# Opening of the first feed-forward part in groups of 2, 3, 4 and 7 row blocks, with every conditioning pass placed behind a low part of the weights

## Chip, cores and metric

The kernel runs on one core of one Trainium2 chip. The metric is the device time of one execution in microseconds, lower is better; three executions of the kernel before give a median of 2366.59 us (2357.86 to 2370.3). Besides these there is one profiled execution, whose trace is read below.

## What is computed

A decoder layer for 256 positions of width 2048: a SwiGLU feed-forward part (width 5632), a pair of token mixers (retention and sliding-window attention), a second feed-forward part, a last norm. Each of the three parts first norms its input and then scales and shifts it by numbers made from a conditioning vector `c`; each result is gated the same way. All weights are fp32 and are used once.

```python
SEQ, D_MODEL, D_FF = 256, 2048, 5632
mod = silu(c) @ w_ada + b_ada            # 9 outputs of 2048: shift, scale, gate for each part
x = x + 0.5 * gate1 * swiglu(modulate(rms_norm(x), shift1, scale1), w_ffn1_gu, w_ffn1_down)
h = modulate(rms_norm(x), shift2, scale2)
x = x + gate2 * token_mixing(h, w_in, w_ret_branch, w_swa_branch, w_out)
x = x + 0.5 * gate3 * swiglu(modulate(rms_norm(x), shift3, scale3), w_ffn2_gu, w_ffn2_down)
return rms_norm(x)
```

(The lines are condensed from the reference.)

## The kernel before

**Weights.** A weight load puts 4 row blocks of 128 by 512 columns (128x2048 numbers, 1 MB) into a buffer `raw`; there are four of them. `load` (L351) issues it on SP's queue. A load is used in two *pieces* of 2 row blocks. For each piece ScalarE (ACT) casts the high part `wh` (`split`, L375), VectorE (DVE) subtracts to get the low part `wl` (L377), and TensorE (PE) does 12 matmuls (`products`, L360): activations high by weights high, low by high, high by low, for 2 row blocks and 2 halves of the positions. The pool that holds `wh` and `wl` has three buffers of each. A `raw` comes free when the low parts of both its pieces are made.

**Conditioning.** One output of `w_ada` (m = 0 to 8) is a sum over 16 rows (k = 0 to 15), each of 128x2048 numbers or 1 MB. A row is loaded on SP's queue (`ada_load`, L215) and multiplied by `silu(c)` and summed on DVE in quarters (`ada_pass`, L220: one pass over 128x512 and a short instruction that reads the sum). Outputs 1 and 0 are needed at once; the others are made later by the generator `conditioning`: after each piece `tick` adds the rate to a counter and takes as many *steps* as are due; a step is one quarter pass, and it asks for the loads of the rows that lie up to `ahead` steps ahead. For outputs 2, 4 and 3 that makes 192 steps; during the rest of the first feed-forward part (`ffn_up`, `down_product`) 1.094 steps come to a piece. During the mixing they are 0.95 to a piece (outputs 7, 6, 5), and in the second feed-forward part 0.43 (output 8). Rows go into a *ring* of two (`two_rows`): row i takes the half that row i-2 had, so its load must wait for the last quarter pass of row i-2.

**What sets the order.** SP's queue is in the order of the program (`manual_schedule`), and an instruction of it that waits holds up everything behind it, weights too. The other engines are ordered by a scheduler, which may pull an instruction ahead of its place in the program; `tc.issue_after(x)` keeps an instruction behind `x`.

**Opening.** The first feed-forward part needs shift and scale of all 16 row blocks of its input. Its first 16 weight chunks (`chunks`) are therefore visited four times, each time with a group of row blocks whose shift and scale are done (`bounds`, `group`, `visit`); meanwhile `group` makes those of the next. Between visits the partial sums lie in SBUF: ACT moves them there (`to_parts`, L1219) and seeds PSUM with them at the next visit (`open_banks`, L1191).

The profile shows these times of the stages: groups at 27 to 65, 65 to 155, 155 to 286 and 286 to 373 us; the rest of the first feed-forward part to about 740 us; then the mixing, in which rows in the ring `rows_x` are used from 1140.1 to 1486.2 us.

Of the kernel before, what the change touches and what calls it, by code (L numbers as in the profile page):

```python
# [9 lines left out]
F32 = mybir.dt.float32  # L10
# [3 lines left out]
ALU = mybir.AluOpType  # L14
# [3 lines left out]
P = 128  # L18
# [59 lines left out]
def layer_kernel(  # L78
# [55 lines left out]
    def t512():  # L134
        return tmp.tile([P, CH], F32, tag="t512", name=nm("t"))
# [4 lines left out]
    def slot():  # L140
        return slots.tile([P, KD * S], F32, tag="slot", name=nm("slot"))
# [69 lines left out]
    def ada_load(m, k, w, loads=1):  # L211
        src = w_ada[(m * KD + k) * P : (m * KD + k + 1) * P, :]
        for i in range(loads):
            at = slice(i * D // loads, (i + 1) * D // loads)
            nc.sync.dma_start(w[:, at], src[:, at])  # L215

    def ada_pass(k, w, sums, q, passes=AQ):

        at = slice(q * D // passes, (q + 1) * D // passes)
        nc.vector.tensor_tensor_reduce(  # L220
            out=w[:, at],
            in0=w[:, at],
            in1=cact[:, at],
            scale=1.0,
            scalar=0.0,
            op0=ALU.mult,
            op1=ALU.add,
            accum_out=sums[:, k, q : q + 1],
        )
# [17 lines left out]
    def raw_row():  # L247
        raw = raws.tile([P, KB, CH], F32, tag="raw", name=nm("raw"))
        return raw.rearrange("p k n -> p (k n)")

    def two_rows(both=None):

        both = slot() if both is None else both
        turn = [both[:, :D], both[:, D:]]

        def place():
            turn.append(turn.pop(0))
            return turn[-1]

        return place  # L260
# [5 lines left out]
    def conditioning(outputs, place, behind):  # L266


        tiles = [(m, k) for m, _, _ in outputs for k in range(KD)]
        held = {}  # L270
        step = 0
# [361 lines left out]
    def parts_of_h(held, k, h):  # L633

        h = h.rearrange("p (k s) -> p k s", s=S)
        nc.scalar.copy(held.hi[:, k : k + 2, :], h)
        nc.vector.tensor_sub(held.lo[:, k : k + 2, :], h, held.hi[:, k : k + 2, :].bitcast(F32))

    def add_gated(bank, t, c0, gate, ssq):

# [338 lines left out]
    rows_of, alone = {}, [False]  # L979

    def place(m, k):
        if k < 1:
            rows_of[m, k] = raw_row()
        else:
            if not alone[0]:
                ring.reverse()
            rows_of[m, k] = ring[0]
        ada_load(m, k, rows_of[m, k], 2 if k < 2 else 1)

# [33 lines left out]
            op0=ALU.mult, op1=ALU.add, accum_out=dest,  # L1023
        )

    def turned_x(k0):

        xn = [t512()[:, : 2 * P] for _ in range(NT)]
        for t in range(NT):
            nc.scalar.mul(xn[t], x_sb[:, t, k0 * P : (k0 + 2) * P], r[:, t : t + 1])  # L1030
        turned = [bank()[:, :S] for _ in range(2)]
        for i in range(2):
# [22 lines left out]
    def normed_columns(k0):  # L1055

        xt = t512()
        both = xt.rearrange("p (k s) -> p k s", s=S)
        nc.sync.dma_start(both, x_t[k0 : k0 + 2].rearrange("k p s -> p k s"))
        nc.gpsimd.tensor_tensor(  # L1060
            out=both, in0=both, in1=root_row[0][:, None, :].broadcast_to([P, 2, S]), op=ALU.mult
        )
        return [xt[:, i * S : (i + 1) * S] for i in range(2)]

    def group(ks, passes=2):

        for k0 in ks[::2]:
            srcs = normed_columns(k0) if k0 >= TURNED else None
            for k in (k0, k0 + 1):
                for m in (1, 0):  # L1070
                    if (m, k) not in rows_of:
                        place(m, k)
                    for q in range(passes):
                        ada_pass(k, rows_of[m, k], early[m], q, passes)
                    yield
            for m in (1, 0):
                ada_end(m, slice(k0, k0 + 2), early[m], 0 if m else None, passes)
            h = t512()
            for i, src in enumerate(srcs or turned_x(k0)):
                modulated(h[:, i * S : (i + 1) * S], k0 + i, src, 0)  # L1080
            parts_of_h(held, k0, h)

    banks, moved, unlinted, fresh = {}, set(), set(), set()
    for n, one_bank in zip(firsts, (acc_bank, side_bank)):
        banks[n] = [one_bank() for _ in range(NT)]

# [17 lines left out]
    with tc.manual_schedule(engines=ORDERED):  # L1104
# [87 lines left out]

    def visit(n, ks, ends, ticks=False, ends_all=False):
        if n not in prepared:
            begin(n, ks)
        if n not in banks:
            open_banks(n, not ends_all)
        for make, part in prepared.pop(n):
            a, b = part[0] - ks[0], part[-1] + 1 - ks[0]
            hl = slice(part[0], part[-1] + 1)  # L1200
            wh, wl = make()
            products(
                banks[n],
                held.hi[:, hl, :],
                held.lo[:, hl, :],
                wh,
                wl,
                n in fresh and a == 0,
                b == len(ks) and ends,
                seeded=n in unlinted,  # L1210
            )
            if ticks:
                tick()
        fresh.discard(n)

    def to_parts(n):
        for p, b in zip(part_of(n), banks.pop(n)):
            with tc.issue_after(cast[-1]):
                nc.scalar.copy(p, b)  # L1219
        moved.add(n)  # L1220

    ROWS_FFN1 = [(2, None, 0.5), (4, 1, None), (3, None, None)]
# [2 lines left out]
    def place_row():  # L1225
        return row_ring[0]() if row_ring else raw_row()

    def place_early():
        if row_ring:
            return row_ring[0]()  # L1230
        return ring[1] if alone[0] else raw_row()

    for g, ks in enumerate(groups):
        alone.append(g == len(groups) - 2)
        del alone[:-1]
# [533 lines left out]
```

## Time and profile before

| | before |
|---|---|
| three executions: median (range) | 2366.59 us (2357.86 to 2370.3) |
| profiled execution: time / span | 2357.64 us / 2355.5 us |
| granted TensorE clock | 0.999 |
| instructions PE matmul / DVE / ACT | 10445 / 2576 / 1888 |
| HBM read over the span | 598.47 MB |
| conditioning rows loaded: into slots / `rows_x` / `raw` | 87 / 31 / 22 |

The page gives for each engine its busy time within the span; the span is what the profiler recorded of the execution, and the time of the execution lies 2.1 us above it. The longest idle times of the other engines (ACT's cast waiting for PE: 752.6 us in 555 waits) are those of engines that run ahead and wait for buffers.

### The profile page before, as it was taken

Reading aid. Unit: us, or ns where it says so; the run is one execution under the profiler, and the core shown is the slowest. Engines: PE = TensorE matmul, PEld = TensorE weight load, DVE = VectorE, ACT = ScalarE, POOL = GpSimd, SP = SyncE. Lnnn points to the kernel's source line nnn. Section 1 sums busy time; section 2 is a strip of 40 time slices with the busy share of each in tenths; the row PEclk is TensorE's granted clock in tenths of the full one; section 3 lists DMA queues with packets and bytes.
Section 4 is the critical chain, followed back from the end, with each engine's and each line's share of the span. In section 5 each row is a group of like instructions: output and inputs, shape, how many; then the busy total and the mean of one; then the engine's idle time right before and its main releaser. Section 6 shows DMA issues by size and latency. Waiting matters only on the chain.

```text
span 2355.5 us, 28357 instructions
## 1 busy us (share of the span) xinstructions
PE 2335.7 (99%) x10445; PEld 1918.6 (81%) x10445; DVE 1673.1 (71%) x2576; ACT 1367.2 (58%) x1888; POOL 18.3 (1%) x27
## 2 busy tenths in 40 slices
PE   8999999999999999999999999999999999999998
PEld 5888888888888888778888888888888888888887
DVE  7788888778867768976777776676555555555656
ACT  6766567455556567774556564465455454455544
POOL 0000000000000000000000000000000000000000
PEclk9999999999999999999999999999999999999999
DMA  9989889988765889876778787754767768666553
GB/s 383 375 323 361 355 294 328 336 306 293 302 237 220 293 267 255 258 212 254 267 273 306 288 310 281 272 204 179 259 237 256 242 239 268 223 231 202 193 197 125
DMA packets 191901, 630.24 MB, mean 268 GB/s; under 512 B 113105, under 2 KB 114769, under 8 KB 121233
## 3 DMA queue, kind: packets, MB, share of 16 engines
q1 hardware_dynamic: 189266, 617.41, 74.6%
q0 software_dynamic: 1600, 9.83, 1.0%
q8 instruction: 82, 1.34, 0.2%
q10 hardware_dynamic: 896, 1.19, 0.1%
q14 instruction: 57, 0.47, 0.1%
HBM read 598.47 MB, written 4.22 MB: 256 GB/s over the span
## 4 chain that ended last, share of the span: by engine, by line
PE 96%; DMA 2%; DVE 1%; ACT 1%; issue 0%; SPq 0%; DVEq 0%; ACTq 0%
PE pa L360 93%; DMA raw<-in_w_ffn_gu_dram 1%; DMA rows_x<-in_w_ada_dram 1%; PE ps L1453 0%; DVE slot L220 0%; PE pd L1369 0%; DVE wl L377 0%; ACT wh L375 0%; DMA x_sb<-in_x_dram 0%; PE ps L360 0%; PE pa L1099 0%; PE ps L895 0%; PE pd L1099 0%; DVE rows_x L220 0%; PE ps L1369 0%
## 5 line engine op out<-in xcount | busy, mean ns | idle before, releaser
L377 DVE TENSOR_TENSOR wl<-raw,wh 128x1024 fp32r<-128x1024 f32 x792 | 963.5, 1225 | 511.0 <-ACT wh L375 451.6
L375 ACT CAST wh<-raw 128x1024 fp32r<-128x1024 f32 x792 | 830.6, 1054 | 818.7 <-PE pa L360 752.6
L360 PE MATMUL pa<-wh,hh 128*128 128x512 f32 x2184 | 597.0, 391 | 3.0 <-ACT wh L375 1.7
L360 PE MATMUL pa<-wh,hl 128*128 128x512 f32 x2184 | 592.6, 389 | 0.0
L360 PE MATMUL pa<-wl,hh 128*128 128x512 f32 x2184 | 586.2, 390 | 0.2
L360 PEld LDWEIGHTS pa<-wh,hh 128*128 128x128 f32 x2184 | 407.5, 188 | 91.6 <-ACT wh L375 2.9
L360 PEld LDWEIGHTS pa<-wl,hh 128*128 128x128 f32 x2184 | 409.4, 188 | 86.7 <-DVE wl L377 1.0
L360 PEld LDWEIGHTS pa<-wh,hl 128*128 128x128 f32 x2184 | 409.8, 188 | 86.1 <-issue 0.4
L360 PE MATMUL pa<-wh,a 128*128 128x512 f32 x1824 | 452.1, 389 | 0.0
L360 PEld LDWEIGHTS pa<-wh,a 128*128 128x128 f32 x1824 | 341.7, 188 | 70.6
L360 PE MATMUL pa<-wl,a 128*128 128x512 f32 x912 | 245.1, 389 | 0.0
L220 DVE CUSTOM_DVE_ANT_0 slot<-slot,cact 128x512 f32<-128x512 f32 (+2 forms) x288 | 219.3, 812 | 30.0 <-DMA slot<-in_w_ada_dram 29.5
L360 PEld LDWEIGHTS pa<-wl,a 128*128 128x128 f32 x912 | 171.1, 188 | 35.4
L551 ACT COPY slot<-back 128x512 uint16<-128x512 uint16 x148 | 98.7, 766 | 0.0
L220 DVE CUSTOM_DVE_ANT_0 rows_x<-rows_x,cact 128x512 f32<-128x512 f32 x124 | 78.7, 686 | 18.0 <-DMA rows_x<-in_w_ada_dram 17.8
L410 ACT CAST a<-slot 128x512 fp32r<-128x512 f32 x114 | 70.6, 620 | 29.3 <-PE pa L360 29.0
L535 ACT COPY flat<-t 128x512 uint16<-128x512 uint16 x136 | 76.7, 617 | 8.9 <-DVE t L1526 5.7
L411 DVE TENSOR_TENSOR a<-slot,a 128x512 fp32r<-128x512 f32 x114 | 77.8, 684 | 0.3 <-ACT a L410 0.3
L220 DVE CUSTOM_DVE_ANT_0 raw<-raw,cact 128x512 f32<-128x512 f32 (+1 forms) x92 | 60.7, 709 | 14.6 <-DMA raw<-in_w_ada_dram 14.5
L1219 ACT COPY slot<-pa 128x512 f32<-128x512 f32 x72 | 38.6, 589 | 21.2 <-PE pa L360 21.0
L360 PE MATMUL pa<-wh,home 128*128 128x512 f32 x160 | 39.5, 389 | 0.0
L220 DVE DVE_READ_ACCUMULATOR2_ANT sums<- 128x1 f32 x440 | 35.9, 82 | 0.0
(232 smaller groups left out, 1087.0 us busy)
## 6 DMA issues: line engine op xcount, KB each, us to landing
raw<-in_w_ffn_gu_dram SPq DMA_DIRECT2D x160, 1024.0 KB, 5.5
raw<-in_w_in_dram SPq DMA_DIRECT2D x104, 1024.0 KB, 5.8
raw<-in_w_ffn_down_dram SPq DMA_DIRECT2D x88, 1024.0 KB, 4.9
slot<-in_w_ada_dram SPq DMA_DIRECT2D x87, 1024.0 KB, 7.4
rows_x<-in_w_ada_dram SPq DMA_DIRECT2D x31, 1024.0 KB, 7.1
raw<-in_w_ada_dram SPq DMA_DIRECT2D x22, 1024.0 KB, 5.7
raw<-in_w_swa_branch_dram SPq DMA_DIRECT2D x16, 1024.0 KB, 5.0
raw<-in_w_ret_branch_dram SPq DMA_DIRECT2D x16, 1024.0 KB, 5.4
```

Of the source, the lines that this page charges most:

```text
L220: nc.vector.tensor_tensor_reduce(out=w[:, at], in0=w[:, at], in1=cact[:, at], scale=1.0, scalar=0.0, op0=ALU.mult, op1=ALU.add, accum_out= ...
L360: product = nc.tensor.matmul(banks[t], act[:, j, t * P : (t + 1) * P], weights[:, j, :], start=starts and i == 0 and j == 0, stop=ends and ...
L375: cast.append(nc.scalar.copy(hi, src).ins)
L377: low.append(nc.vector.tensor_sub(lo, src, hi.bitcast(F32)).ins)
L410: nc.scalar.copy(hi, v)
L411: nc.vector.tensor_sub(lo, v, hi.bitcast(F32))
L535: nc.scalar.copy(planes[:, i, :], words(src)[:, :, i])
L551: nc.scalar.copy(into[:, :, :, i], held["turned"][:, i])
L1219: nc.scalar.copy(p, b)
```

## The change

The groups become 2, 3, 4 and 7 row blocks, so a group may end in a single block, and a weight load in a piece of half the size. Rows of the opening get a slot of their own (`rows_home`), whose two halves always take turns. In the second group chunks 4, 7, 10 and 13 (`by_vector`; chunk 1 is also in the list, but its sums stay in PSUM) are not seeded: DVE adds the old sum afterwards. The later conditioning starts only in the last group, with half-row loads into a ring of four places, and from there on each of its passes, in the whole kernel, is placed behind `low[-1]`, the low part made last in the program's order.

```diff
-    def two_rows(both=None):
+    def two_rows(both=None, parts=2):
         both = slot() if both is None else both
-        turn = [both[:, :D], both[:, D:]]
+        n = 2 * D // parts
+        turn = [both[:, i * n : (i + 1) * n] for i in range(parts)]
+        if parts == 2:
+            turn.reverse()
...
+        def ask(at):
+            (m, k), q = tiles[at // AQ], at % AQ
+            w = place()
+            n = min(w.shape[1] * AQ // D, AQ - q)
+            w = w[:, : n * D // AQ]
+            c0 = q * D // AQ
+            nc.sync.dma_start(
+                w, w_ada[(m * KD + k) * P : (m * KD + k + 1) * P, c0 : c0 + n * D // AQ]
+            )
+            for i in range(n):
+                held[at + i] = (w, q)
+            return n
...
-                    for i in range(step // AQ, min((step + pace["ahead"]) // AQ + 1, len(tiles))):
-                        if i not in held:
-                            held[i] = place()
-                            ada_load(*tiles[i], held[i])
-                    if behind is not None and step < 2 * AQ:
-                        with tc.issue_after(behind.ins):
-                            ada_pass(k, held[step // AQ], sums, q)
-                    else:
-                        ada_pass(k, held[step // AQ], sums, q)
+                    while asked <= step + pace["ahead"] and asked < AQ * len(tiles):
+                        asked += ask(asked)
+                    w, first = held.pop(step)
+                    early_on = behind is not None and step < 2 * AQ
+                    with tc.issue_after(behind.ins if early_on else low[-1]):
+                        ada_pass(k, w, sums, q, first=first)
...
     part = [slot() for _ in range(3)]
-    tiles = [slot(), part[0]]
-    ring = [tiles[0][:, :D], tiles[0][:, D:]]
+    tiles = part[:2]
+    rows_home = slot()
+    ring = [rows_home[:, :D], rows_home[:, D:]]
...
-            if not alone[0]:
-                ring.reverse()
+            ring.reverse()
...
-    TURNED = 6
+    TURNED = 5
...
-    bounds = (0, 2, 6, 12, 16)
+    bounds = (0, 2, 5, 9, 16)
...
+        if seeded and n in by_vector:
+            added.add(n)
+            seeded = False
...
-        for make, part in prepared.pop(n):
+        for i, (make, part) in enumerate(prepared.pop(n)):
+            if ticks and i == KB // 2:
+                turn_step()
...
     def to_parts(n):
         for p, b in zip(part_of(n), banks.pop(n)):
+            if n in added:
+                with tc.issue_after(low[-1]):
+                    nc.vector.tensor_add(p, p, b)
+                continue
...
-        if g == len(groups) - 2:
-            set_pace(ROWS_FFN1, 192, place_early, 0)
+        by_vector = chunks[1::3] if g == 1 else ()
         if final:
-            pace["rate"], pace["ahead"] = 1.0, 1
+            row_ring.append(two_rows(rows_home, 4))
+            set_pace(ROWS_FFN1, 192, place_row, AQ)
...
-            visit(n, ks, n not in stay, g == len(groups) - 2 or final and i < 8, final or (g == len(groups) - 2 and n in stay))
+            visit(n, ks, n not in stay, final, final or (g == len(groups) - 2 and n in stay))
...
-    row_ring.append(two_rows())
+    row_ring[0] = two_rows(rows_home)
     pace["rate"] = (192 - 64) / 117
     pace["ahead"] = AQ
```

What is left out lets `group`, `turned_x`, `normed_columns` and `parts_of_h` take one block in place of two. After the change line 220 is 222, 351 is 368, 375 is 392, 377 is 394, 411 is 428, and the later rows are loaded by `ask` at L285 (those of the opening still at L215).

**VectorE in `down_product` of the first feed-forward part.** `wl` is a low part; a row with a slot and `cact` is a quarter pass, and the 128x1 row behind it reads its sum. The slot named is the ring. Before:

```order
L377 TENSOR_TENSOR wl_795_4545<-raw_793_4542,wh_794_4544 128x1024
L411 TENSOR_TENSOR a_787_4503<-slot_5_114,a_787_4503 128x512
L377 TENSOR_TENSOR wl_797_4563<-raw_793_4542,wh_796_4562 128x1024
L220 ISA slot_562_3115,sums_759_4330<-slot_562_3115,cact_103 128x512
L220 ISA sums_759_4330 128x1
L220 ISA slot_562_3115,sums_759_4330<-slot_562_3115,cact_103 128x512
L220 ISA sums_759_4330 128x1
L220 ISA slot_562_3115,sums_759_4330<-slot_562_3115,cact_103 128x512
L220 ISA sums_759_4330 128x1
L220 ISA slot_562_3115,sums_759_4330<-slot_562_3115,cact_103 128x512
L220 ISA sums_759_4330 128x1
L377 TENSOR_TENSOR wl_802_4588<-raw_800_4585,wh_801_4587 128x1024
```

And now:

```order
L394 TENSOR_TENSOR wl_771_4293<-raw_769_4290,wh_770_4292 128x1024
L222 ISA slot_8_117,sums_599_3229<-slot_8_117,cact_103 128x512
L222 ISA sums_599_3229 128x1
L394 TENSOR_TENSOR wl_773_4310<-raw_769_4290,wh_772_4309 128x1024
L222 ISA slot_8_117,sums_599_3229<-slot_8_117,cact_103 128x512
L222 ISA sums_599_3229 128x1
L428 TENSOR_TENSOR a_774_4327<-slot_5_114,a_774_4327 128x512
L394 TENSOR_TENSOR wl_778_4336<-raw_776_4333,wh_777_4335 128x1024
L222 ISA slot_8_117,sums_599_3229<-slot_8_117,cact_103 128x512
L222 ISA sums_599_3229 128x1
```

Before, the scheduler put the four passes of a row together, some eight pieces ahead of their place in the program; now each stands behind the low part that it has in the program, one to a piece.

**SP's queue in the same stretch.** A row with `w_ada` is a row load, one with `w_ffn1_down` a weight load; the brackets name what it waits for beyond what the queue has waited for already (DMAHW a DMA, DVE and Activation the engine's progress). Before:

```order
L351 DMA raw_736_4172<-in_w_ffn1_down_dram 128x2048 [waits DMAHW2_49,DVE_49]
L215 DMA slot_562_3115<-in_w_ada_dram 128x2048 [waits DMAHW3_49]
L351 DMA raw_742_4213<-in_w_ffn1_down_dram 128x2048 [waits DMAHW5_49,DMAHW4_49,DVE_49]
L215 DMA slot_562_3115<-in_w_ada_dram 128x2048 [waits DMAHW0_49]
L351 DMA raw_749_4256<-in_w_ffn1_down_dram 128x2048 [waits DMAHW7_49,DMAHW6_49,DVE_49]
L351 DMA raw_754_4292<-in_w_ffn1_down_dram 128x2048 [waits DMAHW1_49,DVE_49]
L215 DMA slot_562_3115<-in_w_ada_dram 128x2048 [waits DMAHW3_49]
```

And now:

```order
L368 DMA raw_750_4163<-in_w_ffn1_down_dram 128x2048 [waits DMAHW1_49,Activation_49]
L285 DMA slot_8_117<-in_w_ada_dram 128x2048 [waits DMAHW2_49,DVE_49]
L368 DMA raw_755_4200<-in_w_ffn1_down_dram 128x2048 [waits DMAHW3_49,Activation_49]
L368 DMA raw_763_4249<-in_w_ffn1_down_dram 128x2048 [waits DMAHW4_49,Activation_49]
L285 DMA slot_8_117<-in_w_ada_dram 128x2048 [waits DMAHW5_49,DVE_49]
L368 DMA raw_769_4290<-in_w_ffn1_down_dram 128x2048 [waits DMAHW7_49,DMAHW6_49,Activation_49]
```

The loads stand in the same pattern, one row to two weights (to one, now and then). What moved is the wait on DVE: before it stood at the weight loads, for the low parts that free a `raw`; now it stands at the row loads, for the last pass of the row two before.

**SP's queue in the mixing**, where rows go into `rows_x`; `back` is a transpose by DMA. Before:

```order
L215 DMA rows_x_9224<-in_w_ada_dram 128x2048 [waits DMAHW2_49]
L351 DMA raw_1778_10171<-in_w_swa_branch_dram 128x2048 [waits DMAHW3_49,DVE_49]
L351 DMA raw_1784_10214<-in_w_swa_branch_dram 128x2048 [waits DMAHW4_49,DVE_49]
L215 DMA rows_x_9224<-in_w_ada_dram 128x2048 [waits DMAHW5_49]
L540 DMA_TRANSPOSE back_1789_10251<-flat_1749_10033 128x8x128 [waits DMAHW6_49,Activation_49]
```

And now:

```order
L285 DMA rows_x_9301<-in_w_ada_dram 128x2048 [waits DMAHW4_49,DVE_49]
L368 DMA raw_1805_10248<-in_w_swa_branch_dram 128x2048 [waits DMAHW5_49,Activation_49]
L368 DMA raw_1811_10291<-in_w_swa_branch_dram 128x2048 [waits DMAHW6_49,Activation_49]
L285 DMA rows_x_9301<-in_w_ada_dram 128x2048 [waits DMAHW7_49,DVE_49]
L557 DMA_TRANSPOSE back_1816_10328<-flat_1776_10110 128x8x128 [waits DMAHW0_49,Activation_49]
```

Here too the wait on DVE has gone from the weights to the rows.

More of the change, by code (lines that the diff above doesn't have):

```diff
@@ L215, in ada_load, with ada_pass @@
             nc.sync.dma_start(w[:, at], src[:, at])
-    def ada_pass(k, w, sums, q, passes=AQ):
-        at = slice(q * D // passes, (q + 1) * D // passes)
+    def ada_pass(k, w, sums, q, passes=AQ, first=0):
+        n = D // passes
+        at = slice(q * n, (q + 1) * n)
+        here = w[:, (q - first) * n : (q + 1 - first) * n]
         nc.vector.tensor_tensor_reduce(
-            out=w[:, at],
-            in0=w[:, at],
+            out=here,
+            in0=here,
             in1=cact[:, at],
@@ L270, in conditioning @@
         held = {}
-        step = 0
+        step = asked = 0
+        def ask(at):
[10 more added lines that the diff above has]
+            return n
         for m, gain, row in outputs:
@@ L635, in parts_of_h @@
         h = h.rearrange("p (k s) -> p k s", s=S)
-        nc.scalar.copy(held.hi[:, k : k + 2, :], h)
-        nc.vector.tensor_sub(held.lo[:, k : k + 2, :], h, held.hi[:, k : k + 2, :].bitcast(F32))
+        ks = slice(k, k + h.shape[1])
+        nc.scalar.copy(held.hi[:, ks, :], h)
+        nc.vector.tensor_sub(held.lo[:, ks, :], h, held.hi[:, ks, :].bitcast(F32))
     def add_gated(bank, t, c0, gate, ssq):
@@ L978, in layer_kernel @@
     early = [ada_sums() for _ in range(2)]
-    rows_of, alone = {}, [False]
+    rows_of = {}
     def place(m, k):
@@ L1024, in square, with turned_x @@
         )
-    def turned_x(k0):
-        xn = [t512()[:, : 2 * P] for _ in range(NT)]
+    def turned_x(k0, nk=2):
+        xn = [t512()[:, : nk * P] for _ in range(NT)]
         for t in range(NT):
-            nc.scalar.mul(xn[t], x_sb[:, t, k0 * P : (k0 + 2) * P], r[:, t : t + 1])
-        turned = [bank()[:, :S] for _ in range(2)]
-        for i in range(2):
+            nc.scalar.mul(xn[t], x_sb[:, t, k0 * P : (k0 + nk) * P], r[:, t : t + 1])
+        turned = [bank()[:, :S] for _ in range(nk)]
+        for i in range(nk):
             for t in range(NT):
@@ L1053, in roots_in_rows, with normed_columns @@
         nc.scalar.copy(root_row[0], rows_ps[:, :S])
-    def normed_columns(k0):
-        xt = t512()
+    def normed_columns(k0, nk):
+        xt = t512()[:, : nk * S]
         both = xt.rearrange("p (k s) -> p k s", s=S)
-        nc.sync.dma_start(both, x_t[k0 : k0 + 2].rearrange("k p s -> p k s"))
+        nc.sync.dma_start(both, x_t[k0 : k0 + nk].rearrange("k p s -> p k s"))
         nc.gpsimd.tensor_tensor(
-            out=both, in0=both, in1=root_row[0][:, None, :].broadcast_to([P, 2, S]), op=ALU.mult
+            out=both, in0=both, in1=root_row[0][:, None, :].broadcast_to([P, nk, S]), op=ALU.mult
         )
-        return [xt[:, i * S : (i + 1) * S] for i in range(2)]
+        return [xt[:, i * S : (i + 1) * S] for i in range(nk)]
     def group(ks, passes=2):
         for k0 in ks[::2]:
-            srcs = normed_columns(k0) if k0 >= TURNED else None
-            for k in (k0, k0 + 1):
+            nk = min(2, ks[-1] + 1 - k0)
+            srcs = normed_columns(k0, nk) if k0 >= TURNED else None
+            for k in range(k0, k0 + nk):
                 for m in (1, 0):
@@ L1076, in group @@
             for m in (1, 0):
-                ada_end(m, slice(k0, k0 + 2), early[m], 0 if m else None, passes)
-            h = t512()
-            for i, src in enumerate(srcs or turned_x(k0)):
+                ada_end(m, slice(k0, k0 + nk), early[m], 0 if m else None, passes)
+            h = t512()[:, : nk * S]
+            for i, src in enumerate(srcs or turned_x(k0, nk)):
                 modulated(h[:, i * S : (i + 1) * S], k0 + i, src, 0)
             parts_of_h(held, k0, h)
-    banks, moved, unlinted, fresh = {}, set(), set(), set()
+    banks, moved, unlinted, fresh, added = {}, set(), set(), set(), set()
     for n, one_bank in zip(firsts, (acc_bank, side_bank)):
```

7 lines of the change are left out of this document (1 added, 6 removed).

## The prediction

> **What bounds the kernel now.** I read the page's head and busy times first, then the chain of work that ended last, then the windows of busy time by stage. The page:
>
> ```profile
> span 2355.5 us, 28357 instructions
> PE 2335.7 (99%) x10445; PEld 1918.6 (81%) x10445; DVE 1673.1 (71%) x2576; ACT 1367.2 (58%) x1888; POOL 18.3 (1%) x27
> PE 96%; DMA 2%; DVE 1%; ACT 1%; issue 0%; SPq 0%; DVEq 0%; ACTq 0%
> ```
>
> PE is busy for all but 2355.5 - 2335.7 = 19.8 us, and the chain is 96% PE. The windows (columns: stretch, length, then busy time and instructions of each engine, granted clock, DMA share and rate) show where these 19.8 us lie. The first three are from the opening, then two from the rest of the first feed-forward part, then one from the mixing:
>
> ```profile
> 0.00:27.00 27.00, 18.57 (x31) 7.73 (x31) 17.51 (x45) 13.46 (x28) 2.01 (x8) 1.00 0.95 365
> 27.00:65.00 38.00, 36.21 (x159) 28.18 (x158) 31.95 (x37) 28.09 (x45) 0.00 (x0) 1.00 0.99 382
> 155.00:286.00 131.00, 130.49 (x576) 107.65 (x575) 108.34 (x189) 77.75 (x108) 4.25 (x2) 1.00 0.88 346
> 480.00:600.00 120.00, 120.00 (x531) 99.37 (x531) 93.35 (x163) 63.67 (x75) 0.00 (x0) 1.00 0.82 302
> 600.00:740.00 140.00, 140.00 (x619) 115.98 (x618) 106.13 (x159) 77.24 (x97) 0.54 (x1) 1.00 0.72 268
> 1200.00:1350.00 150.00, 150.00 (x663) 124.28 (x662) 111.34 (x185) 88.65 (x110) 0.00 (x0) 1.00 0.83 299
> ```
>
> The start, before the first group, has 27 - 18.57 = 8.4 us of them, the first group 1.8, the third 0.5. From 480 to 740 us and in the mixing PE never stops. So the change can win little (19.8 - 8.4 = 11.4 us if all idle time behind the start went), and what it can lose is cover that exists now. The chain's longest piece gives PE's rate:
>
> ```profile
> 63.87 158.08 PE pa L360 x696
> ```
>
> 158.08 / 696 = 0.227 us a matmul, so **a piece of 12 is 2.725 us of PE**.
>
> **What the change does, part by part.** *The hold, in the rest of the first feed-forward part.* Before, the four passes of a row ran together as soon as it had landed. The timeline there (start, length, engine, line; SPq are DMA issues):
>
> ```profile
> 425.69 0.33 SPq L351 DMA_DIRECT2D raw<-in_w_ffn_gu_dram  x1
> 426.07 0.42 SPq L215 DMA_DIRECT2D slot<-in_w_ada_dram  x1
> ...
> 427.20 1.23 DVE L377 TENSOR_TENSOR wl<-raw,wh 128x1024 fp32r<-128x1024 f32 x1 [1.54 <-ACT wh L375]
> ...
> 428.34 0.68 DVE L220 CUSTOM_DVE_ANT_0 slot<-slot,cact 128x512 f32<-128x512 f32 x1
> ...
> 428.95 0.08 DVE L220 DVE_READ_ACCUMULATOR2_ANT sums<- 128x1 f32 x1
> 428.95 0.69 DVE L220 CUSTOM_DVE_ANT_0 slot<-slot,cact 128x512 f32<-128x512 f32 x1
> ```
>
> A low part holds DVE for 428.34 - 427.20 = 1.14 us, a quarter pass for 428.95 - 428.34 = 0.61, the pair 1.75. Because the passes ran early, the ring's half was long free when SP came to the next row load, and weights were issued when a `raw` came free, about six pieces before their cast. Line 351 from 373 to 720 us, who waited for it and its time to landing, then line 215 there:
>
> ```profile
>   ACT wh L375: 2.1, 1
> ...
> DMA to landing us min/median/max: 4.7/5.0/14.1
> ```
> ```profile
> DMA to landing us min/median/max: 6.8/7.9/14.4
> ```
>
> One wait for a weight in 347 us. A load alone needs 4.7 us or more; a row, issued right behind a weight, 6.8 or more.
>
> Now the order puts one pass behind each low part. Following the two queues through this stretch, SP's row load i waits for the last pass of row i-2, one or two pieces ahead of the first weight behind it. That weight used to have six. The loop that follows, counted from the release: row issue 0.42 us, the weight behind it 6.8 (second in the queue, as the row was; I take the lowest, since a starved queue holds nothing else), the cast 1.05 from its row,
>
> ```profile
> L375 ACT CAST wh<-raw 128x1024 fp32r<-128x1024 f32 x792 | 830.6, 1054 | 818.7 <-PE pa L360 752.6
> ```
>
> and 0.1 for the handoffs: **8.4 us until DVE can make that weight's first low part**, then 1.75 for each low part and pass until the one that releases the next row. In 22 pieces the order has six such cycles, with 3, 3, 2, 2, 2 and 1 pairs: 6 x 8.4 + 13 x 1.75 = 73.2 us against 22 x 2.725 = 60.0 on PE. Every cycle is longer than its pieces (three pairs: 13.65 for 10.9), so PE's backlog helps once and not each time. Loss 13.2 us per 22 pieces; the stretch with such row loads is 106 pieces, so 106 / 22 x 13.2 = 64, less a backlog of two pieces (5.5 us; three buffers of `wl` would be 8.2, none 0): **+58 us**.
>
> *The hold in the mixing* (ring `rows_x`). The rows of that tile, its loads and their landing:
>
> ```profile
> L215 SPq DMA_DIRECT2D rows_x<-in_w_ada_dram x31: 372/425/1174, 1130.8 to 1477.6; - x31
> ...
> DMA to landing us min/median/max: 6.8/7.1/10.2
> ```
>
> The order has 24 cycles over 101 pieces there, 65 pairs in all: 24 x 8.4 + 65 x 1.75 = 315.4 against 275.2, +40.1; for the 29 rows of 31 that wait for a half, x 29/24 = 48.5, less a backlog of 5.5: **+43 us**. Around `rows_x`, where rows go into `raw` at the start of the mixing, and in the second feed-forward part (a row per 9.4 pieces), the order leaves two to four pieces, and the pieces between two rows give the backlog back: nothing, with at most one late weight of 8.4 + 1.75 - 2 x 2.725 = 4.7 us at each end.
>
> *The opening.* Before the third group stood almost without stops although its weights came just in time. The groups by line, form kept apart, 155 to 286 us:
>
> ```profile
> L377 DVE TENSOR_TENSOR wl<-raw,wh 128x1024 fp32r<-128x1024 f32 x48 | 59.4, 1254 | 21.5 <-ACT wh L375 21.4
> ...
> L375 ACT CAST wh<-raw 128x1024 fp32r<-128x1024 f32 x49 | 51.1, 1052 | 53.3 <-DMA raw<-in_w_ffn_gu_dram 33.2 <-PE pa L360 18.3 <-DVE wl L377 1.7
> ```
>
> The cast waited for weights for 33.2 us there, yet PE lost 0.5: late casts are covered as long as they come before PE. After the change the third group must load 14 rows, one beside each weight load of two pieces: 2.1 MB in 5.45 us, 385 GB/s. The first group ran at 382 with DMA engines 99% busy, the old third at 346. At 382 a row's turn takes 5.49 us (14 x 0.04 = 0.6 us lost), at 346 it takes 6.06 (8.5 lost); I take 1, by the first group, which also runs rows beside weights. The ring's release stands four to five pieces (10.9 us) ahead there, enough for 8.4. The first group gets 6 rows in place of 8 and may win its 1.8 us, and the third loses its wait of 0.5: net -1.
>
> *By vector.* Eight additions from PSUM on DVE take the place of eight seeds and eight moves on ACT. The nearest row of DVE with a PSUM operand (from 373 to 700 us):
>
> ```profile
> L710 DVE TENSOR_TENSOR t<-t,pa 128x512 f32<-128x512 f32 x6 | 3.8, 679 | 0.0
> ```
>
> 8 x 0.68 = 5.4 us of DVE beside a second group that gives it slack; nothing on the path, 5.4 if uncovered, -1 if a seed had held PE. Half pieces (32 more casts and low parts, no more matmuls), half-row loads and the extra `turn_step` go the same way: DVE and ACT have room, 0 to 3 us.
>
> **Sum**: 2355.5 - 1 + 58 + 43 = 2455.5, and the 2.1 us around the span make 2457.6, **2458 us**, against 2357.64 of the profiled execution. The median of the three runs lies 9 us above that execution; I stay on its side.
>
> A fixed price for transfers gives a little less. The Trainium skill, "DMA: Bandwidth & Descriptors", section "Anatomy of one DMA", fits 2.0 us plus bytes at 436 GB/s, given for loads that GpSimd issues: 4.4 us for 1 MB, and 2.4 more for a second behind it, 6.8. The trace's lowest values are 4.7 and 6.8; where the medians of the trace (7.1, 7.9) hold, the loop is longer.
>
> **Rivals.**
>
> 1. *Only one stretch starves* (2358 + 58 = 2416 or 2358 + 43 = 2401). For it: in the mixing the order has transposes and softmax between; against: they make the loop longer.
>
> 2. *Nothing starves: 2350 to 2362, not slower.* DVE may run up to three `wl` buffers ahead of PE, so a release that is one piece ahead in DVE's order would be four ahead in PE's, 10.9 us for a need of 8.4, and the cover would hold. It decides if the weight lands within 10.9 - 5.25 - 1.2 = 4.5 us of the release (three pairs per cycle). Against it: the lowest landing of a load alone is 4.7, and here a row goes ahead; and DVE's lead is eaten by the same loop. That the hold does nothing is excluded by the order.
>
> 3. *Faster.* The opening loses its waits; all idle time behind the start, 11.4 us, gives 2346, and a change of 0.5% (11.8 us, about what a measurement of this kernel can tell) isn't reached.
>
> 4. *Much slower.* If landings are the medians, 7.1 and 7.9 in place of 6.8, the 58 cycles add 17 to 64 us: 2475 to 2520. Or PE itself slows in the new gaps. The start shows slow matmuls beside idle time (groups by line, 0 to 66 us):
>
> ```profile
> L360 PE MATMUL pa<-wh,hl 128*128 128x512 f32 x49 | 13.3, 391 | 0.0
> ...
> L1099 PE MATMUL pa<-raw,t 128*128 128x512 f32 x8 | 5.7, 847 | 1.8 <-ACT t L628 1.8
> ```
>
> 847 ns for the shape that later takes 391. If each of 58 gaps cost six matmuls at 2 x 0.227, 58 x 6 x 0.227 = 79 us came on top where PE, not the loop, is last: up to 2537. My gaps are 1.4 to 2.8 us (10.15 for 8.2 or 13.65 for 10.9 in DVE's loop), spread over several casts, and the loop, not PE, sets the pace. The skill's "TensorE: Matmul & The Clock Gate", section "Part 1: The HAM clock gate", wants an idle window of about 3.4 us before the clock halves; by that these gaps would not do it, and no stretch before the change has such gaps to show it.
>
> **How the numbers follow.** Both stretches starve as worked out (2430 to 2480): 0.62. The fourth rival, 2480 to 2537: 0.13. One stretch alone, or both with a larger backlog (2390 to 2430): 0.13. Nothing: 0.09. Faster: 0.03. From the first three: slower by over 0.5% 0.88, within 0.5% 0.09, faster 0.03. The range, 2398 to 2505, takes in one stretch alone and the 7.1 us landing, and leaves out the second and third rivals and the upper part of the fourth.
>
> **What would show it.** Right: PE's busy share falls from 1.00 to about 0.8 in the windows from 390 to 690 us and near 0.87 from 1140 to 1490; ACT's cast waits for `raw` loads for tens of us; row issues follow the end of a pass, and the weights behind them land about 7.2 us later. The stretch from 740 to 1130 us and the end stay as long as before. Wrong: PE stays at 0.99 in these windows (second rival), the weight lands under 5 us after the row's issue, or the opening is late by more than 8 us.

## The result, and the profile after

The changed kernel takes 2516.76 us (median of 6, 2513.33 to 2520.07) against 2359.6 us of the kernel before (median of 6, 2356.95 to 2370.3): a ratio of 1.0666, 95% interval 1.0648 to 1.0684. It is slower, as forecast, by 157 us where 100 were forecast, and 12 us above the range. The page of the changed kernel:

```profile
span 2512.6 us, 28462 instructions
PE 2379.9 (95%) x10443; PEld 1934.0 (77%) x10443; DVE 1677.6 (67%) x2610; ACT 1354.0 (54%) x1889; POOL 19.1 (1%) x28
...
PE 47%; DMA 6%; DVE 2%; ACT 2%; issue 1%; SPq 1%; ACTq 0%; DVEq 0%
```

The chain could be followed back only to 996 us here, so its shares add up to 59% and not to 100. DVE and ACT do about the same work as before (1677.6 and 1354.0 us busy, 1673.1 and 1367.2 before), yet PE is no longer always busy. The windows show where (columns as before: stretch, length, busy time of PE, PEld, DVE, ACT, POOL, granted clock, DMA share and rate). First the opening, then the rest of the first feed-forward part, then the mixing, and last a stretch of the mixing in the kernel before:

```profile
27.00:65.00 38.00, 37.24 (x166) 29.76 (x165) 30.15 (x35) 29.79 (x49) 0.00 (x0) 1.00 0.92 347
65.00:155.00 90.00, 89.50 (x395) 73.81 (x394) 74.98 (x109) 64.69 (x100) 6.26 (x4) 1.00 0.93 354
155.00:286.00 131.00, 131.00 (x580) 108.51 (x579) 115.67 (x192) 85.24 (x120) 3.36 (x2) 1.00 0.92 342
...
480.00:600.00 120.00, 99.61 (x384) 78.45 (x383) 66.72 (x118) 46.39 (x57) 0.00 (x0) 0.90 0.63 229
600.00:740.00 140.00, 120.93 (x483) 95.52 (x482) 90.57 (x154) 57.16 (x72) 0.00 (x0) 0.93 0.60 230
```
```profile
1240.00:1450.00 210.00, 186.81 (x799) 150.76 (x798) 131.31 (x248) 102.41 (x144) 0.00 (x0) 0.98 0.63 228
1450.00:1640.00 190.00, 165.89 (x704) 132.94 (x703) 115.74 (x193) 83.24 (x99) 0.00 (x0) 0.98 0.66 247
```
```profile
1240.00:1450.00 210.00, 209.19 (x924) 172.92 (x923) 155.02 (x256) 118.95 (x145) 0.00 (x0) 1.00 0.84 302
```

In the opening PE is busy almost throughout; from 480 to 600 us it did 384 matmuls where before it did 531. DMA is less busy as well (0.63 for 0.82), so it is not bandwidth. How much of the loss lies where can be read from the start of the same low part in both traces (the changed kernel makes 16 more in the opening, so they are matched from the end):

| low part, counted in the changed kernel | after, us | before, us | later by |
|---|---|---|---|
| 150, near the end of the opening's last group | 398.9 | 398.6 | 0.3 |
| 260, end of the rows of the first feed-forward part | 785.4 | 693.7 | 91.7 |
| 403, before `rows_x` | 1261.9 | 1172.0 | 90.0 |
| 535, after `rows_x` | 1692.4 | 1535.1 | 157.2 |
| 799, near the end | 2457.8 | 2300.6 | 157.2 |

So 91 us are lost in the first stretch, about 65 (157.2 - 90.0 = 67, and some 2 us won back just before) in the second, and nothing anywhere else. Line 368 from 385 to 770 us, who waited for its loads and how long these took to land, and the row loads of line 285:

```profile
  ACT wh L392: 137.7, 41
...
DMA to landing us min/median/max: 6.8/7.5/13.1
```
```profile
L285 SPq DMA_DIRECT2D slot<-in_w_ada_dram x29: 327/328/328, 399.0 to 763.9; - x29
...
DMA to landing us min/median/max: 4.8/4.9/5.9
```

Before, the casts waited once for a weight (2.1 us); now 41 times, 137.7 us. One turn of the loop can be read from two views of the changed kernel, SP's timeline and DVE's (start, length, engine, line):

```profile
621.01 0.33 SPq L285 DMA_DIRECT2D slot<-in_w_ada_dram  x1
621.43 0.86 SPq L368 DMA_DIRECT2D raw<-in_w_ffn_down_dram  x2
633.15 0.33 SPq L285 DMA_DIRECT2D slot<-in_w_ada_dram  x1
633.57 0.38 SPq L368 DMA_DIRECT2D raw<-in_w_ffn_down_dram  x1
643.47 0.33 SPq L285 DMA_DIRECT2D slot<-in_w_ada_dram  x1
```
```profile
629.54 1.23 DVE L394 TENSOR_TENSOR wl<-raw,wh 128x1024 fp32r<-128x1024 f32 x1 [1.79 <-ACT wh L392]
630.68 0.69 DVE L222 CUSTOM_DVE_ANT_0 slot<-slot,cact 128x512 f32<-128x512 f32 x1
...
631.29 1.22 DVE L394 TENSOR_TENSOR wl<-raw,wh 128x1024 fp32r<-128x1024 f32 x1
632.43 0.69 DVE L222 CUSTOM_DVE_ANT_0 slot<-slot,cact 128x512 f32<-128x512 f32 x1
633.04 0.09 DVE L222 DVE_READ_ACCUMULATOR2_ANT sums<- 128x1 f32 x1
```

The row goes out at 621.01, the weights right behind it; the first low part of such a weight starts at 629.54, 8.5 us after the row; two pairs later, at 633.13, the last pass is read, and 0.02 us on the next row goes out. SP issued nothing between 622.3 and 633.15. In the mixing the chain itself runs around this loop: from 1301.51 us it goes through a row's issue (L285), the load of the weight behind it (6.83 us), the cast (1.05), the low parts and passes on DVE, and the next row's issue at 1315.27.

### The profile page after: what moved, and what is told of

Read it like the earlier page. It is cut to its first block, busy times and chain, and to the rows that moved or that the text cites. A ratio compares the mean times of both kernels' runs of the same rounds, so it can differ in the third digit from the quotient of the medians.

```text
span 2512.6 us, 28462 instructions
## 1 busy us (share of the span) xinstructions
PE 2379.9 (95%) x10443; PEld 1934.0 (77%) x10443; DVE 1677.6 (67%) x2610; ACT 1354.0 (54%) x1889; POOL 19.1 (1%) x28
## 3 DMA queue, kind: packets, MB, share of 16 engines
q10 hardware_dynamic: 896, 1.19, 0.1%
## 4 chain that ended last, share of the span: by engine, by line
PE 47%; DMA 6%; DVE 2%; ACT 2%; issue 1%; SPq 1%; ACTq 0%; DVEq 0%
PE pa L377 46%; DMA raw<-in_w_in_dram 4%; DMA raw<-in_w_swa_branch_dram 1%; ACT wh L392 1%; DVE wl L394 1%; DMA raw<-in_w_ret_branch_dram 1%; DVE rows_x L222 1%; SPq L557 1%; PE ps L1475 0%; ACT slot L568 0%; PE pd L1391 0%; PE ps L377 0%; SPq L285 0%; DVE soft L1462 0%; PE pd L1560 0%
## 5 line engine op out<-in xcount | busy, mean ns | idle before, releaser
L394 DVE TENSOR_TENSOR wl<-raw,wh 128x1024 fp32r<-128x1024 f32 (+1 forms) x808 | 969.2, 1204 | 632.1 <-ACT wh L392 574.2
L392 ACT CAST wh<-raw 128x1024 fp32r<-128x1024 f32 (+1 forms) x808 | 822.9, 1035 | 847.8 <-PE pa L377 489.1
L377 PE MATMUL pa<-wh,hh 128*128 128x512 f32 x2184 | 604.8, 394 | 58.7 <-ACT wh L392 56.8
L377 PE MATMUL pa<-wh,hl 128*128 128x512 f32 x2184 | 601.7, 392 | 0.0
L377 PE MATMUL pa<-wh,a 128*128 128x512 f32 x1824 | 469.6, 401 | 56.1 <-ACT wh L392 46.2
L377 PEld LDWEIGHTS pa<-wh,a 128*128 128x128 f32 x1824 | 349.0, 193 | 142.4 <-ACT wh L392 57.2
L222 DVE CUSTOM_DVE_ANT_0 slot<-slot,cact 128x512 f32<-128x512 f32 (+2 forms) x310 | 244.8, 800 | 1.7 <-DMA slot<-in_w_ada_dram 1.6
L428 DVE TENSOR_TENSOR a<-slot,a 128x512 fp32r<-128x512 f32 x114 | 78.1, 689 | 69.5 <-ACT a L427 69.1
L222 DVE CUSTOM_DVE_ANT_0 rows_x<-rows_x,cact 128x512 f32<-128x512 f32 x124 | 85.2, 687 | 0.0
L222 DVE CUSTOM_DVE_ANT_0 raw<-raw,cact 128x512 f32<-128x512 f32 (+1 forms) x72 | 51.0, 717 | 0.0
```

The source lines that it names most:

```text
L222: nc.vector.tensor_tensor_reduce(out=here, in0=here, in1=cact[:, at], scale=1.0, scalar=0.0, op0=ALU.mult, op1=ALU.add, accum_out=sums[:, ...
L377: product = nc.tensor.matmul(banks[t], act[:, j, t * P : (t + 1) * P], weights[:, j, :], start=starts and i == 0 and j == 0, stop=ends and ...
L392: cast.append(nc.scalar.copy(hi, src).ins)
L394: low.append(nc.vector.tensor_sub(lo, src, hi.bitcast(F32)).ins)
L428: nc.vector.tensor_sub(lo, v, hi.bitcast(F32))
```

## The experiments

All start from the changed kernel, except the second. "Queue theory" means that a held pass frees the ring late and SP's queue, in order, holds the weights back behind the row. Times of a single execution (those without a ratio) are compared with executions of the kernel before on the same chip (medians 2357.57 to 2358.89 us); the six executions of the changed kernel lie within 6.7 us of each other.

**No hold.**

```diff
-                    with tc.issue_after(behind.ins if early_on else low[-1]):
+                    with tc.issue_after(behind.ins) if early_on else nullcontext():
                         ada_pass(k, w, sums, q, first=first)
```

> The changed kernel with no conditioning pass held behind a low part; the opening in groups of 2, 3, 4 and 7 and all else stay. Queue theory (a held pass frees the ring late, so the weights behind the next row load are issued late): the whole loss goes, 2350 to 2362 us. Rival (the opening or the smaller loads cost as well): between 2370 and 2510 us.

2356.35 us, ratio 0.9977 (0.9961 to 0.9994). The whole loss is the hold's; with the opening in groups of 2, 3, 4 and 7, and all that goes with it, the kernel is 1 to 2 us faster than the one before (medians 2357.66 here and 2358.89 below).

> The changed kernel with no conditioning pass held, a second time and in more rounds: the new opening by itself. Expected 1 to 5 us below the kernel before, a ratio of 0.998 to 1.000, as in its first runs.

2356.53 us, ratio 0.9982 (0.997 to 0.9993).

**The hold alone**, in the kernel before.

```diff
                     else:
-                        ada_pass(k, held[step // AQ], sums, q)
+                        with tc.issue_after(low[-1]):
+                            ada_pass(k, held[step // AQ], sums, q)
```

> The kernel before with nothing but the hold on every later conditioning pass. Queue theory: 91 us in the rest of the first feed-forward part and 65 in the mixing as in the changed kernel, 2500 to 2530 us. In the old third group, where such passes also run, up to 10 us more. Rival (the hold costs only together with the new opening): under 2420 us.

2562.8 us, ratio 1.0855 (1.0803 to 1.0906). The hold needs no help from the new opening. It costs more than I expected, a miss by 33 us above the range: later conditioning already ran in the third group of the old opening, in one half of the ring. The windows of this kernel, third group and after:

```profile
155.00:286.00 131.00, 117.02 (x487) 94.95 (x486) 89.59 (x151) 65.72 (x92) 2.77 (x2) 0.95 0.71 280
286.00:330.00 44.00, 38.37 (x161) 30.93 (x160) 33.61 (x61) 20.02 (x25) 0.00 (x0) 0.96 0.84 317
```

PE did 487 matmuls from 155 to 286 us, 576 in the kernel before: about 20 us. Read from the low parts, some 40 us are lost by the end of the opening, where I had allowed for 10, then 96 in the rest of the first feed-forward part and 72 in the mixing. Why these two lose 5 to 7 us more than in the changed kernel stays open.

**The hold off in the rest of the first feed-forward part only.**

```diff
     row_ring[0] = two_rows(rows_home)
+    pace["hold"] = False
...
+    pace["hold"] = True
     set_pace([(7, 2, None), (6, None, None), (5, None, 1.0)], 192 / 0.95, place_row, 2)
```

> The changed kernel with the hold taken off only from the end of the opening to the end of the first feed-forward part. If the two stretches add up without touching each other: 2517 - 91 = 2426 us (2418 to 2434), PE at 1.00 from 390 to 690 us. Rival (a common cause such as the PE clock over the whole run): the mixing gains too, under 2400 us.

2423.93 us: 93 us less. The two stretches add up.

**Rows on another queue.** The hold stays on every pass; only SP's queue is relieved.

```diff
-            nc.sync.dma_start(
+            pace["queue"].dma_start(
                 w, w_ada[(m * KD + k) * P : (m * KD + k + 1) * P, c0 : c0 + n * D // AQ]
             )
...
     row_ring[0] = two_rows(rows_home)
+    pace["queue"] = nc.gpsimd
...
+    pace["queue"] = nc.sync
     set_pace([(7, 2, None), (6, None, None), (5, None, 1.0)], 192 / 0.95, place_row, 2)
```

> The changed kernel with the hold everywhere, but in the rest of the first feed-forward part the row loads are issued from GpSimd's queue, so a row that waits for its half of the ring holds up no weight load on SP. Queue theory: the 91 us of that stretch go, save what rows that now land late cost DVE (0 to 25 us): 2426 to 2450 us. Rival (the interleaving of passes and low parts on DVE is itself what costs): stays above 2490 us.

2425.45 us, half a microsecond under the range: the 91 us are gone with each pass still behind its low part. The windows of this kernel:

```profile
480.00:600.00 120.00, 120.00 (x531) 99.38 (x530) 94.27 (x164) 64.01 (x76) 6.36 (x12) 1.00 0.88 312
600.00:740.00 140.00, 140.00 (x619) 115.91 (x619) 112.04 (x178) 76.83 (x97) 4.79 (x9) 1.00 0.74 272
```

PE is busy throughout, as before the change. What costs is not the interleaving on DVE but who stands behind the waiting row on SP.

**Rows asked for later.** A row's load stands two steps later in the program, three steps after its half came free.

```diff
-    pace["ahead"] = AQ
+    pace["ahead"] = 2
...
-        pace["ahead"] = AQ
+        pace["ahead"] = 2
```

> The changed kernel with the hold everywhere, but rows are asked for two steps ahead in place of four, in the rest of the first feed-forward part and for rows_x. A row's load then stands two steps later on SP, behind weights that used to wait for it, three steps after its half came free. Queue theory: the weights keep their lead; the row has two steps (5 us) to land and DVE waits up to 2 us a row, which its lead over PE covers: 2355 to 2400 us. Rival (the hold itself costs, wherever the row stands): above 2480 us.

2362.59 us, ratio 1.0003 (0.9983 to 1.0022): two numbers take back all but some 6 us against the kernel without a hold. The casts still wait for weights there, now without harm. Its group of casts from 385 to 740 us and the sum of its windows from 373 to 740:

```profile
L392 ACT CAST wh<-raw 128x1024 fp32r<-128x1024 f32 x126 | 130.9, 1053 | 130.5 <-PE pa L377 75.5 <-DMA raw<-in_w_ffn_gu_dram 27.6 <-DMA raw<-in_w_ffn_down_dram 23.7
```
```profile
sum 367.00, PE 363.52 PEld 298.72 DVE 282.35 ACT 192.39 POOL 2.17; mean PE 121.17 PEld 99.57 DVE 94.12 ACT 64.13 POOL 0.72
```

51 us of waiting for weights, and PE idle for 3.5 us of 367: nearly all of these waits fall into ACT's lead over PE.

**A ring of four half rows.**

```diff
-    row_ring[0] = two_rows(rows_home)
+    row_ring[0] = two_rows(rows_home, 4)
...
-        row_ring.append(two_rows(one.tile([P, 2 * D], F32, tag="x", name="rows_x")))
+        row_ring.append(two_rows(one.tile([P, 2 * D], F32, tag="x", name="rows_x"), 4))
```

> The changed kernel with the hold everywhere, but the ring of these two stretches has four places of half a row, in the same memory, loaded by half. A half row is asked for four steps ahead and its place came free three steps before. Queue theory: the weights keep a lead of four to five pieces, 2352 to 2370 us. Rival (the hold itself costs): above 2480 us; rival (twice as many loads, of half the size, cost time on SP or in the transfer): 2380 to 2420 us.

2369.29 us, ratio 1.0038 (1.0022 to 1.0054). Where the new ring takes over, its first load overwrites half a row that is still to be used, so one conditioning output differs from the reference's. The loss is gone here too, up to 13 us against the kernel without a hold; whether these come from twice as many loads was not separated.

**Is it PE's clock?** The granted clock fell to 0.90 in the stretch. From 373 to 740 us the sums of the windows, after and before, are:

```profile
sum 367.00, PE 311.18 PEld 246.30 DVE 220.94 ACT 144.14 POOL 2.16; mean PE 103.73 PEld 82.10 DVE 73.65 ACT 48.05 POOL 0.72
```
```profile
sum 367.00, PE 367.00 PEld 304.08 DVE 281.92 ACT 202.36 POOL 0.54; mean PE 122.33 PEld 101.36 DVE 93.97 ACT 67.45 POOL 0.18
```

1257 matmuls (390 + 384 + 483) in 311.18 us are 0.248 us each; 0.225 would make 283. So 28 of the 84 us that are missing look like slow matmuls, a rival that my fourth case had named. Two kernels change PE's work and nothing else:

```diff
+                    if extra[0] and i == 0 and not starts and j < extra[0]:
+                        nc.tensor.matmul(
+                            banks[t],
+                            al[:, j, t * P : (t + 1) * P],
+                            weights[:, j, :],
+                            start=False,
+                            stop=False,
+                            skip_group_check=seeded,
+                        )
...
+    extra[0] = 1
```

> The changed kernel with the hold everywhere and two matmuls more in each piece of the rest of the first feed-forward part (low activations by the first high block are added twice, so the sums there differ a little): 100 pieces x 2 x 0.227 = 45 us more of PE work. Loop theory (PE has slack in each cycle): 0 to 20 us more, 2517 to 2537 us. Rival (PE at its lower clock is what comes last there): 45 us more or above, 2560 us and over. If the lower clock comes from the gaps and costs time by itself: less than 2510 us, since the gaps get shorter.

2538.36 us, 22 more: 1 us above what the loop theory allowed, and far below the rival. Read from the low parts, the stretch itself grew by 10 us (low part 249: 85.9 us later than before the change, now 95.6), and 13 came after it (low parts 249 to 282), where nothing holds PE and each extra matmul counts.

```diff
+        less[0] -= 1
...
+                    if less[0] >= 0 and i == 1 and j == 1:
+                        continue
...
+    less[0] = 100
```

> The changed kernel with the hold everywhere and two matmuls fewer in each of the first 100 pieces after the opening (low activations by high weights are left out for one of two row blocks): 45 us less of PE work, all of it within the stretch that loses 91 us. Loop theory (DMA, cast, low part and pass set the pace there): 0 to 10 us less, 2507 to 2517 us. Rival (PE at its lower clock comes last): 45 us less or more, 2472 us or under.

2517.89 us, no less at all (1 us above the range of the loop theory, 46 above the rival's), though the clock there was lower still (sums of the same windows of this kernel):

```profile
480.00:600.00 120.00, 90.35 (x327) 70.10 (x326) 66.64 (x119) 46.77 (x58) 0.00 (x0) 0.86 0.64 226
...
sum 367.00, PE 277.70 PEld 215.35 DVE 217.72 ACT 144.04 POOL 2.16; mean PE 92.57 PEld 71.78 DVE 72.57 ACT 48.01 POOL 0.72
```

PE worked 33 us less and the program ended at the same time. So the slow matmuls mostly fill time in which PE would have waited; the loop through DMA, ACT and DVE sets the end.

**A shorter loop.** A row load brings half of a row, then a quarter; the waits and the order stay.

```diff
+            e = n * D // AQ // pace["share"]
             nc.sync.dma_start(
-                w, w_ada[(m * KD + k) * P : (m * KD + k + 1) * P, c0 : c0 + n * D // AQ]
+                w[:, :e], w_ada[(m * KD + k) * P : (m * KD + k + 1) * P, c0 : c0 + e]
             )
...
-                held[at + i] = (w, q)
+                held[at + i] = (w, q + i // 2 * 2 * (pace["share"] - 1))
```

> The changed kernel with the hold everywhere; in the rest of the first feed-forward part a row load brings only the left half of the row (512 KB, and the third and fourth pass go over the same half again), so those conditioning outputs are not computed; the waits, the order and the number of loads stay. Loop theory (row transfer, weight transfer, cast, low part and passes follow one another): each of 28 cycles is 2.45 us shorter, most fall to PE's pace, and the stretch costs 5 to 30 us in place of 91: 2431 to 2456 us. Rival (the slow PE clock makes the loss, not the length of the loop): over 2480 us.

2495.78 us, 21 less, not 60 to 86: a miss, and by its time alone what the rival said. The landing of the row loads, here and with a quarter row:

```profile
DMA to landing us min/median/max: 3.6/4.2/4.6
```
```profile
DMA to landing us min/median/max: 3.1/3.4/3.7
```

A whole row takes 4.9 (median); half of it saves 0.7 and not 2.45, and the weight behind it came only some half a microsecond earlier. The loop got shorter by 0.40 us on the mean of 28 cycles (13.03 to 12.63), which is 11 of the 21 us; the first of these rows went out 5.7 us earlier besides (393.3 for 399.0).

With a quarter row (the edit is shown against the kernel with half rows):

```diff
-    pace["share"] = 2
+    pace["share"] = 4
...
-                held[at + i] = (w, q + i // 2 * 2 * (pace["share"] - 1))
+                held[at + i] = (w, q + i if pace["share"] > 1 else q)
```

> As the kernel with half rows, but a row load of the rest of the first feed-forward part brings only the first quarter of the row (256 KB; all four passes go over it, so those conditioning outputs are not computed). With half rows the 28 cycles were 0.40 us shorter on the mean (13.03 to 12.63) and the time 21 us less, since the weight landed only some 0.5 us earlier, not 2.45. Loop theory: the time follows the first low part of the weight behind the row. A quarter row moves half as much again, so I expect cycles of 12.0 to 12.4 us and a time of 2460 to 2490 us. Rival (the loop's length does not set the time): 2490 to 2500 us whatever the cycles are.

2490.98 us, with cycles of 12.45 us: the weight's first low part came at 7.7 us after the row in place of 8.8 (8.3 with half rows), but the rest of the cycle grew from 4.25 to 4.76. This kernel's waits in the stretch, where the same row of the changed kernel reads 8.7 us in 10 waits:

```profile
ACT wh L393 <- PE pa L378: 18.9, 16, 2.1
```

As the loop gets shorter the casts wait more for PE; that PE's slow matmuls are the reason fits, but no run shows it. By its time this run lies 1 us above the range of the loop theory, inside the rival's, and its cycles just miss theirs, so it speaks for neither; the two with other PE work and the one with rows on another queue separate them.

**The hold in the opening only.**

```diff
     row_ring[0] = two_rows(rows_home)
+    pace["hold"] = False
```

> The changed kernel with the hold only in the last group of the opening, where a place in the ring is asked for three steps after it came free; no hold from the end of the opening on. Queue theory: the last group loses nothing, so the same as without any hold, 2353 to 2360 us. Rival (the hold is of use to the last group, whose DVE is 85% busy): 2 to 5 us faster than without it.

2356.43 us, ratio 0.9977 (0.9965 to 0.999), the same as without any hold. In the last group of the opening, where the ring of four half rows leaves three steps, the hold costs nothing and brings nothing. Of all kernels run, this one and the one without a hold are the fastest, by some 2 us.

## Why the prediction's mechanism was right, and where its size was wrong

- *The mechanism* held: the row's wait moved to SP's queue, the weights behind it lost their lead, and both stretches starve. The hold off in one stretch, the rows on another queue and the rows asked for two steps later each take it away.
- *The places* held: between the two stretches low parts ran up to 7 us later for a while, but none of it stayed, and nothing was lost in the second feed-forward part.
- *The opening*, forecast at -1 us, was right: by 373 us PE has done 9 matmuls more than before (1562 for 1553, 2 us), 7 of them in the first group, and the 14 rows beside the weights of the third group cost no time (PE 131.00 us busy of 131). The eight additions by DVE are hidden: the only wait of PE in the second group, 0.5 us, is for a seed from ACT.
- *"8.4 us until DVE can make that weight's first low part, then 1.75 for each low part and pass"* was too small: this is the step that failed, by size. I had cycles of 73.2 / 6 = 12.2 us; the row loads give (763.9 - 399.0) / 28 = 13.03. In `rows_x` I had 315.4 / 24 = 13.1; there (1652.2 - 1257.7) / 28 = 14.09. That is 28 x 0.83 = 23 us and 28 x 0.95 = 27 of what is missing. The first low part came 8.8 and 9.1 us after the row, on the mean, and the pairs behind it took 4.25 and 5.0 in place of 3.8 and 4.7. I had counted the shortest landing and bare durations. What else stands in the loop wasn't counted: transposes by DMA on SP between a row and its weights (1.7 us before the weight in place of 0.4, three of 28 times), DVE's other work between two low parts (L428, L728), ACT's copies ahead of a cast, and another 0.1 us from the last pass to the next row's issue. How much of the 0.83 each takes was not separated.
- *"Less a backlog of two pieces (5.5 us)"* held in one stretch of two. The 28 cycles of the first take 364.9 us for 102 pieces, 278 us of PE: 87 too long, and 91 were lost. So nothing was covered there, and of the 33 us missing the last 10 are these 5.5 and some 4 at the two ends. In `rows_x` 28 cycles take 394.5 us for 118 pieces, 322 us of PE: 73 too long, and 67 were lost, so about 6 was covered.
- *The range* went to 7.1 us of landing; it didn't allow for the other work in the loop, since the loop was made from durations of a stretch in which none of it was late.
- *The fourth rival* gave the right time (2475 to 2537) for wrong reasons: the weight behind the row landed 6.9 us after its issue at the median, 0.1 over what I took, and the clock, which did fall, cost little time of its own, as the two runs with other PE work show. The 847 ns that it sets beside 391 is a mean of one line's matmuls, which took 1061 ns up to 23.5 us and 592 after it; so the slow ones took 1.8 times as long there, not 2.2 times.

## What to carry to other kernels

Before a wait is put on an engine's instruction, ask which buffer it frees, which load waits for that buffer, and what stands behind this load on an in-order queue: the price is paid there, not on the engine that waits. An instruction that "only goes to its place in the program" gives up the lead that a scheduler had made; asking for the buffer some steps after it comes free restores it. A loop that has become the bound has to be summed with everything that stands in it, at typical durations, not the least; only what is shown to be slack may be left out.

## What the runs showed of the hardware

- A gap of 2.4 us on PE was enough for slow matmuls. From the timeline of the changed kernel:

```profile
485.52 1.56 PE L377 MATMUL pa<-wh,hh 128*128 128x512 f32 x4 [2.42 <-ACT wh L392]
...
486.88 1.91 PE L377 MATMUL pa<-wh,hl 128*128 128x512 f32 x4
...
489.97 1.07 PE L377 MATMUL pa<-wh,hh 128*128 128x512 f32 x4
```

After 2.42 us of idle time four matmuls span 1.91 us where they span 1.07 when PE is kept busy, and after about 4.5 us they are back; from 486.2 to 489.5 us the granted clock reads 0.50. Not every gap of this length does it: after 3.13 us of idle time at 511.80 the next two groups of four span 1.19 and 1.08, and the clock stays at 1.00. The Trainium skill's "TensorE: Matmul & The Clock Gate", section "Part 1: The HAM clock gate", which the prediction cites, has an idle window of about 3.4 us; here a shorter gap did it, and the measurement decides.

- A row load of 1024, 512 and 256 KB, with a weight load issued 0.4 us behind it, takes 4.9, 4.2 and 3.4 us to land (medians): most of the time doesn't go with the size. The first low part of the weight behind it comes 8.8, 8.3 and 7.7 us after the row's issue, so it gains little from a shorter row.
